# Three chunks of 4, 5 and 7 blocks in the input projection, the first norm's root ahead of the conditioning sums, lambdas and bounds at the beginning

## The chip, the cores and the metric

The kernel runs on one core of a Trainium2 chip. The metric is the device time of one execution in microseconds. The kernel before takes 1553.63 us, the median of 3 runs (1551.51 to 1554.83).

## The reference

One encoder layer on 256 rows of width 2048, all in float32:

```
cond = silu(c);  mod = cond @ w_mod + b_mod          # w_mod is 2048 x 12288, 101 MB
sh1, sc1, gt1, sh2, sc2, gt2 = split(mod, 6)
u = rms_norm(x, norm1_g) * (1 + sc1) + sh1
aq|ak|av|rq|rf|ri|rg|ga|gr = u @ w_in                # w_in is 2048 x 11264
lam = exp(sum(lq1*lk1)) - exp(sum(lq2*lk2)) + lam_init
ya = differential attention(aq, ak, av, lam)
yr = gated linear recurrence(rq, rf, ri, rg; lower bounds from softmax(lb_logits))
m = sigmoid(ga) * (ya @ w_att_out) + sigmoid(gr) * (yr @ w_rec_out)
x = x + gt1 * (m @ w_o);  u2 = rms_norm(x, norm2_g) * (1 + sc2) + sh2
x = x + gt2 * ((silu(u2 @ w_ffn_gate) * (u2 @ w_ffn_up)) @ w_ffn_down);  out = rms_norm(x, final_g)
```

Each weight is used once, on 256 rows. The output must hold float32 accuracy, so each matrix product is made of three passes (below).

## The kernel before

Rows of x lie in two halves of 128; the 2048 inputs of each product are 16 blocks of 128. A weight tile w is loaded by a DMA of SP's queue (L220), cast by ScalarE to a rounded high half wh (L235), and VectorE subtracts it to get the low half wl (L237). The activations have halves uH and uL likewise. TensorE then issues three matmuls of 512 columns for each block and each half of the rows: wh with uH, wl with uH, wh with uL (L245 to L247), so 6 matmuls a block, into PSUM tiles named acc.

The first norm needs its scale and shift, which are themselves a product with w_mod (sc1, sh1). VectorE makes them, in mod_cols: tiles wm of w_mod are loaded, multiplied by a column of cond and summed into two tiles modc (L398 and L402; ci is 0 for the shift and 1 for the scale); TensorE sums these over the partitions by matmuls against a column of ones, into pmc (L330; each is two records in the trace); VectorE adds the bias and the norm's weight (sh_col, sc_col, L421 to L423); ScalarE makes u (L368) and uH (L378), VectorE uL (L379).

The first 7 groups of columns of w_in (rf, rq, ri, aq, ak, av, rg, in 14 groups of 512 columns) do not wait for all 16 blocks. The blocks are cut into chunks, kchunks: 3, 4, 5 and 4 blocks (L45). For each chunk all 14 groups are computed with that chunk's blocks alone. After the first chunk ScalarE copies the sums to tiles part (L452); after each later chunk VectorE adds the new sums to them (L454). While chunk n runs, the scale and shift for chunk n+1 are made beside it, spread over the groups by pace["cond"] (AHEAD is 1.15, so a little ahead of even). Chunk 0's are made before anything else. Its wm tiles, and half of the next chunk's, lie in buffers of the big pool (27 of 4 KB a partition); all others share 3 buffers of their own, as the weights w have 3.

Blocks of a chunk beyond a multiple of 4 are loaded apart: 3 blocks in a load of 128x3x512; a single block in a load of 128x1024, shared by two groups.

Ahead of all this the kernel loads c, turns it into columns by TensorE, and makes cond = silu(c) (sigmoid on ScalarE, L131). load_rows loads six small parameters by ScalarE's queue. rstd1 sums the squares of x on ScalarE (L338) and takes the root by Newton steps on VectorE (L350, L198 to L213); norm1 scales x by it (L357), TensorE turns it (L360), ScalarE stores xT (L361). small_params makes lower bounds and lambda; its four loads of lambda stand in SP's queue (L179).

A scheduler of the language orders the instructions of each engine by its own model of times, within the data's dependencies. An engine executes its list in that order and waits at the first instruction that is not ready. tc.issue_after(ins) adds a rule to that ordering: what is issued under it, on the engine of ins, stands behind ins in the list. Each DMA has one of 8 slots (DMAHW0 to DMAHW7), given out in turn to all queues; a DMA waits until the one before it in its slot has landed.

Of the kernel before, what the change touches and what calls it, by code (L numbers as in the profile page):

```python
# [12 lines left out]
AF = mybir.ActivationFunctionType  # L13
# [5 lines left out]
P = 128  # L19
D = 2048  # L20
S = 256
KT = D // P
# [19 lines left out]
UACT, YACT = True, True  # L42
XAT, XAT2 = 2, 14
PACE2, PACE3, PACES, PACE1 = 0.7, 1.6, 2.2, 1.5
kchunks = [(0, 3), (3, 4), (7, 5), (12, 4)]  # L45


AQ, AK, AV, RQ, RF, RI, RG, GA, GR = 0, 1024, 2048, 3072, 4096, 5120, 6144, 7168, 9216
# [3 lines left out]
def block_kernel(  # L52
# [7 lines left out]
    nc = tc.nc  # L60
    x, out = x[0], out[0]
# [16 lines left out]
    def bank(name):  # L78
        return ps.tile([P, 512], F32, tag="ps", name=name)

    def tmpt(name, n=512, dt=F32):
        return tmp.tile([P, n], dt, tag=f"t{n}", name=name, bufs={512: NT, 256: 2}[n])
# [39 lines left out]
    def quarter(tiles, g):  # L122

        return tiles[g // 2][:, (g % 2) * NG:(g % 2 + 1) * NG]
# [3 lines left out]
    pcond = bank("pcond")  # L128
    nc.tensor.transpose(out=pcond[:, :KT], in_=crow[:KT, :], identity=ident[:KT, :KT])
    cond = const.tile([P, KT], F32, name="cond")  # L130
    nc.scalar.activation(cond, pcond[:, :KT], AF.Sigmoid)  # L131
    nc.vector.tensor_mul(out=cond, in0=cond, in1=pcond[:, :KT])

    nrow, nbrow = 57, 6 * KT
# [2 lines left out]
    g1c, g2c, lbl, gnc = cols[:, 0:16], cols[:, 16:32], cols[:, 32:48], cols[:, 48:56]  # L137
# [24 lines left out]
    def small_params():  # L162

        m8 = small.tile([P, HEADS], F32, tag="s8", name="lbm")
        nc.vector.tensor_max(out=m8, in0=lbl[:, 0:8], in1=lbl[:, 8:16])
        e = small.tile([P, 2, HEADS], F32, tag="s16", name="lbe")
        for i in range(2):
            nc.vector.tensor_sub(out=e[:, i], in0=lbl[:, 8 * i:8 * i + 8], in1=m8)
        nc.scalar.activation(e, e, AF.Exp)
        z = small.tile([P, HEADS], F32, tag="s8", name="lbz")  # L170
        nc.vector.tensor_add(out=z, in0=e[:, 0], in1=e[:, 1])
        nc.vector.reciprocal(out=z, in_=z)
        nc.vector.tensor_mul(out=lbc, in0=e[:, 0], in1=z)
        nc.vector.tensor_scalar(out=omlb, in0=lbc, scalar1=-1.0, scalar2=1.0, op0=ALU.mult, op1=ALU.add)
        nc.vector.tensor_scalar_mul(out=subc, in0=cols[:, 56:57], scalar1=1.0 - LAM_INIT)

        lv = tmpt("lv", S).rearrange("p (i d) -> p i d", d=64)
        for i, ap in enumerate((lambda_q1, lambda_q2, lambda_k1, lambda_k2)):
            nc.sync.dma_start(out=lv[:, i, :], in_=ap.to_broadcast([P, 64]))  # L179
        nc.vector.tensor_mul(out=lv[:, 0:2], in0=lv[:, 0:2], in1=lv[:, 2:4])  # L180
        ls = small.tile([P, 2], F32, tag="s2", name="ls")
        nc.vector.reduce_sum(out=ls, in_=lv[:, 0:2], axis=AX.X)
        nc.scalar.activation(ls, ls, AF.Exp)

        nc.vector.tensor_sub(out=lam[:, 0:1], in0=ls[:, 0:1], in1=ls[:, 1:2])
        nc.vector.tensor_scalar_add(out=lam[:, 0:1], in0=lam[:, 0:1], scalar1=LAM_INIT)
        nc.vector.tensor_scalar_mul(out=lam[:, 1:2], in0=lam[:, 0:1], scalar1=-1.0)

    last_rstd = []
# [110 lines left out]
    def halves(tiles):  # L300

        return lambda k, ts: tiles[k // 4].rearrange("p (k s) -> p k s", s=S)[:, k % 4, ts]
# [34 lines left out]
    def square_sum(dst, src):  # L337
        return nc.scalar.activation(junk[:, :src.shape[-1]], src, AF.Square, accum_out=dst)  # L338

    xT, uH_t, uL_t = [], [], []  # L340
    xTv, uH, uL = halves(xT), halves(uH_t), halves(uL_t)

    def rstd1(xt):

        s8 = small.tile([P, 2, 4], F32, tag="s8", name="ssq")
        for t in range(2):
            for g in range(4):
                square_sum(s8[:, t, g:g + 1], quarter(xt[t], g))
        s2 = small.tile([P, 2], F32, tag="s2", name="ssq1")
        nc.vector.reduce_sum(out=s2, in_=s8, axis=AX.X)  # L350
        return rstd_of(s2, 2, D, "n1")
# [29 lines left out]
    def mod_loads(nk):  # L381
        wid = nk * P
        kk = min(KT, 1024 // wid)
        return [(q, min(kk, KT - q)) for q in range(0, KT, kk)]

    def mod_cols(k0, nk, chunk, gcol, src, H, L, after=None, room=0, lag=0):

        wid = nk * P  # L390
        a = [tmp.tile([P, 1024], F32, tag="modc", name=f"modc{ci}", bufs=2) for ci in range(2)]
        waiting = []

        def sums(q, kk, ci, w):
            for j in range(kk):
                s1, d = cond[:, q + j:q + j + 1], a[ci][:, :wid]
                if q + j == 0:
                    first = nc.vector.tensor_scalar_mul(out=d, in0=w[:, j], scalar1=s1)  # L398
                    if after is not None:
                        tc.add_manual_dep(first.ins, after.ins.name, NOSYNC, reason="the norm goes first")  # L400
                else:
                    nc.vector.scalar_tensor_tensor(out=d, in0=w[:, j], scalar=s1, in1=d, op0=ALU.mult, op1=ALU.add)  # L402

        for q, kk in mod_loads(nk):
            for ci in range(2):
                waiting.append((q, kk, ci, load_mod(q, kk, (chunk + ci) * D + k0 * P, wid, q >= room)))
                if ci == 0:
                    yield
            while len(waiting) > (lag if q < room else 0):
                sums(*waiting.pop(0))  # L410
            yield
        for w in waiting:
            sums(*w)
        p = bank("pmc")
        for ci in range(2):
            col_sum(p, ci * nk, a[ci], nk)
        for _ in range(GAP if chunk else GAP1):
            yield
        ks = slice(k0, k0 + nk)
        bc = [bcols[:, (chunk + ci) * KT + k0:(chunk + ci) * KT + k0 + nk] for ci in range(2)]  # L420
        nc.vector.tensor_add(out=sh_col[:, ks], in0=p[:, 0:nk], in1=bc[0])  # L421
        nc.vector.tensor_add(out=sc_col[:, ks], in0=p[:, nk:2 * nk], in1=bc[1])
        nc.vector.scalar_tensor_tensor(out=sc_col[:, ks], in0=sc_col[:, ks], scalar=1.0, in1=gcol[:, ks], op0=ALU.add, op1=ALU.mult)  # L423
        if src is not None:
            for k in range(k0, k0 + nk):
                modulated(src(k, slice(0, S)), k, H, L)
# [30 lines left out]

    def mods1(ci):
        k0, nk = kchunks[ci]
        return mod_cols(k0, nk, 0, g1c, xTv, uH, uL, room=(KT, KT // 2, 0, 0)[ci], lag=(0, 4, 0, 0)[ci])  # L460

    def chunk_cols(ci):
        k0, nk = kchunks[ci]
# [166 lines left out]
    def attention(hh):  # L630
# [6 lines left out]
        for t in range(2):  # L637
# [50 lines left out]
            yield  # L688

    first = mods1(0)  # L690
    for _ in range(XAT):
        next(first)
    x1 = load_x()
    load_rows()
    r1 = rstd1(x1)
    for _ in range(XAT2):
        next(first, None)
    xT += bigt("xT", n=4)
    for g in range(4):
        norm1(x1, r1, g)  # L700
# [4 lines left out]
    for ci in range(len(kchunks)):  # L705
        chunk_cols(ci)
        if ci == 0:
            small_params()
            make_masks()


# [213 lines left out]
```

## Time and profile before

| what | value |
| --- | --- |
| median of 3 runs | 1553.63 us |
| profiled execution: time, span | 1557.73 us, 1555.5 us |
| TensorE matmul busy | 1504.1 us (97%) |
| VectorE busy | 1101.3 us (71%) |
| ScalarE busy | 733.9 us (47%) |
| moved by DMA | 373.67 MB, mean 240 GB/s |

The span is the time from the first to the last instruction of the profiled execution. Matmuls are pipelined, so a busy TensorE is not one at its peak: starts have to be counted. A group of instructions goes by its line in the kernel, the engine and the operation. The name in brackets behind an idle time is what ended the wait, by the semaphores.

### The profile page before, as it was taken

What the parts mean: (1) busy time and instruction counts of PE and PEld (TensorE: products, weight loads), DVE (VectorE), ACT (ScalarE), POOL (GpSimd) and SP (SyncE); (2) the same over time, 40 slices, a digit from 0 to 9 for tenths busy, and PEclk for the clock granted to TensorE, in tenths of its full rate; (3) what the DMA queues carried; (4) which work ended last, traced back from release to release, by engine and by line L of the source; (5) the groups of instructions that cost most, each with busy time, mean ns of one, the idle gap of its engine ahead of it and who ended that gap; (6) DMA issues with size and microseconds to landing.
All of it is one profiled execution on the core that took longest, in us unless ns stands there. A gap on an engine that the chain in (4) does not pass through costs nothing.

```text
span 1555.5 us, 18285 instructions
## 1 busy us (share of the span) xinstructions
PE 1504.1 (97%) x6931; PEld 1236.5 (79%) x6931; DVE 1101.3 (71%) x1439; ACT 733.9 (47%) x1016; POOL 10.5 (1%) x40
## 2 busy tenths in 40 slices
PE   3999999999999999999989999999999999999997
PEld 2778788888878778788878888888888888888885
DVE  5879898688877687988469878879555555555555
ACT  5653433524566764444355555444433444444443
POOL 1000000000000000000000000000000000000000
PEclk9999999999999999999999999999999999999998
DMA  9789898634664379899549998958655555556553
GB/s 319 268 296 338 276 322 289 208 126 158 228 246 160 111 279 323 317 323 339 194 145 333 329 323 288 317 195 312 214 191 190 190 188 190 190 189 210 196 192 105
DMA packets 175986, 373.67 MB, mean 240 GB/s; under 512 B 8429, under 2 KB 12694, under 8 KB 175898
## 3 DMA queue, kind: packets, MB, share of 16 engines
q1 hardware_dynamic: 175352, 371.90, 69.6%
q8 instruction: 54, 0.88, 0.2%
q10 hardware_dynamic: 546, 0.61, 0.1%
q14 instruction: 34, 0.28, 0.0%
HBM read 370.38 MB, written 2.10 MB: 239 GB/s over the span
## 4 chain that ended last, share of the span: by engine, by line
PE 79%; DVE 9%; DMA 6%; ACT 2%; issue 2%; SPq 0%; DVEq 0%; ACTq 0%
PE acc L246 24%; PE acc L247 24%; PE acc L245 24%; DMA wm<-in_w_mod_dram 5%; DVE wl L237 3%; DVE modc L402 2%; PE ptr L499 2%; PE pl L584 2%; PE pmc L330 1%; DVE gt L315 1%; DMA w<-in_w_in_dram 1%; DMA x<-in_x_dram 1%; DVE part L454 0%; ACT wh L235 0%; PE psc L647 0%
## 5 line engine op out<-in xcount | busy, mean ns | idle before, releaser
L235 ACT CAST wh<-w 128x1024 fp32r<-128x1024 f32 (+1 forms) x518 | 528.8, 1030 | 669.3 <-PE acc L247 568.0
L237 DVE TENSOR_TENSOR wl<-w,wh 128x1024 fp32r<-128x1024 f32 (+1 forms) x518 | 614.2, 1193 | 325.0 <-ACT wh L235 323.3
L246 PE MATMUL acc<-wl,uH 128*128 128x512 f32 x704 | 278.2, 395 | 2.0 <-DVE wl L237 2.0
L245 PE MATMUL acc<-wh,uH 128*128 128x512 f32 x704 | 276.8, 396 | 3.2 <-ACT uH L378 1.9
L247 PE MATMUL acc<-wh,uL 128*128 128x512 f32 x704 | 277.4, 394 | 0.0
L246 PE MATMUL acc<-wl,u2H 128*128 128x512 f32 x704 | 274.4, 390 | 2.8 <-DVE wl L237 2.8
L245 PE MATMUL acc<-wh,u2H 128*128 128x512 f32 x704 | 275.3, 391 | 1.6 <-ACT u2H L786 1.6
L247 PE MATMUL acc<-wh,u2L 128*128 128x512 f32 x704 | 274.9, 391 | 0.0
L402 DVE SCALAR_TENSOR_TENSOR modc<-wm,cond,modc 128x512 f32<-128x512 f32 (+3 forms) x210 | 168.1, 822 | 18.4 <-DMA wm<-in_w_mod_dram 17.5
L246 PEld LDWEIGHTS acc<-wl,uH 128*128 128x128 f32 x704 | 133.3, 189 | 33.5 <-DVE wl L237 5.3
L245 PEld LDWEIGHTS acc<-wh,uH 128*128 128x128 f32 x704 | 133.3, 189 | 30.8 <-ACT uH L378 2.0
L246 PEld LDWEIGHTS acc<-wl,u2H 128*128 128x128 f32 x704 | 132.2, 188 | 31.0 <-DVE wl L237 3.6
L247 PEld LDWEIGHTS acc<-wh,uL 128*128 128x128 f32 x704 | 133.2, 189 | 28.0 <-issue 0.6
L245 PEld LDWEIGHTS acc<-wh,u2H 128*128 128x128 f32 x704 | 132.2, 188 | 29.1 <-ACT u2H L786 1.9
L247 PEld LDWEIGHTS acc<-wh,u2L 128*128 128x128 f32 x704 | 132.2, 188 | 27.1 <-DVE u2L L787 0.2
L246 PE MATMUL acc<-wl,fH 128*128 128x512 f32 x352 | 137.4, 390 | 0.0
L247 PE MATMUL acc<-wh,fL 128*128 128x512 f32 x352 | 137.1, 390 | 0.0
L245 PE MATMUL acc<-wh,fH 128*128 128x512 f32 x352 | 137.0, 389 | 0.0
L315 DVE SCALAR_TENSOR_TENSOR gt<-wm,cond,gt 128x1024 f32<-128x1024 f32 x64 | 81.7, 1277 | 11.8 <-DMA wm<-in_w_mod_dram 11.5
L247 PEld LDWEIGHTS acc<-wh,fL 128*128 128x128 f32 x352 | 66.1, 188 | 14.0 <-issue 0.2
L246 PEld LDWEIGHTS acc<-wl,fH 128*128 128x128 f32 x352 | 66.1, 188 | 13.8 <-issue 0.2
L245 PEld LDWEIGHTS acc<-wh,fH 128*128 128x128 f32 x352 | 66.1, 188 | 13.7
(251 smaller groups left out, 1226.6 us busy)
## 6 DMA issues: line engine op xcount, KB each, us to landing
wm<-in_w_mod_dram SPq DMA_DIRECT2D x160, 512.0 KB, 6.2
w<-in_w_in_dram SPq DMA_DIRECT2D x74, 1024.0 KB, 5.5
w<-in_w_ffn_gate_dram SPq DMA_DIRECT2D x44, 1024.0 KB, 5.2
w<-in_w_ffn_up_dram SPq DMA_DIRECT2D x44, 1024.0 KB, 7.3
w<-in_w_ffn_down_dram SPq DMA_DIRECT2D x44, 1024.0 KB, 5.2
w<-in_w_o_dram SPq DMA_DIRECT2D x16, 1024.0 KB, 7.2
w<-in_w_in_dram SPq DMA_DIRECT2D x14, 768.0 KB, 7.7
wm<-in_w_mod_dram SPq DMA_DIRECT2D x32, 320.0 KB, 4.3
```

The lines of the kernel that those rows point to most:

```text
L235: nc.scalar.copy(out=wh, in_=src)
L237: nc.vector.tensor_sub(out=wl, in0=src, in1=wh.bitcast(F32))
L245: mm(po[t], aH(k, ts), h, start=first, stop=False)
L246: mm(po[t], aH(k, ts), lo, start=False, stop=False)
L247: mm(po[t], aL(k, ts), h, start=False, stop=last)
L315: nc.vector.scalar_tensor_tensor(out=a[i], in0=w[:, 0], scalar=cond[:, k:k + 1], in1=a[i], op0=ALU.mult, op1=ALU.add)
L330: mm(p[:, j0 + j:j0 + j + 1], a[:, j * P:(j + 1) * P], ones[:, 0:1], start=True, stop=True)
L402: nc.vector.scalar_tensor_tensor(out=d, in0=w[:, j], scalar=s1, in1=d, op0=ALU.mult, op1=ALU.add)
L499: nc.tensor.transpose(out=p[:, j * P:(j + 1) * P], in_=src[:, j * P:(j + 1) * P], identity=ident)
L584: mm(p[:, (4 * b + j) * 64:(4 * b + j + 1) * 64], kb[:, j, b * P:(b + 1) * P], qb[:, j, b, :, 1, :], start=True, stop=True)
```

## The change

The chunks become 4, 5 and 7 blocks instead of 3, 4, 5 and 4. The first norm's squares are issued behind the sigmoid on ScalarE; the conditioning sums from the third step of the generator on are issued behind the last Newton step on VectorE. small_params is split: lambdas() loads the lambdas by ScalarE's queue instead of SP's and makes lambda, small_params() the bounds; both are called ahead of norm1, under the same rule, instead of behind the first chunk.

```diff
-kchunks = [(0, 3), (3, 4), (7, 5), (12, 4)]
+kchunks = [(0, 4), (4, 5), (9, 7)]
...
-    nc.scalar.activation(cond, pcond[:, :KT], AF.Sigmoid)
+    cond_act = nc.scalar.activation(cond, pcond[:, :KT], AF.Sigmoid)
...
         nc.vector.tensor_scalar_mul(out=subc, in0=cols[:, 56:57], scalar1=1.0 - LAM_INIT)
 
+    def lambdas():
+
         lv = tmpt("lv", S).rearrange("p (i d) -> p i d", d=64)
         for i, ap in enumerate((lambda_q1, lambda_q2, lambda_k1, lambda_k2)):
-            nc.sync.dma_start(out=lv[:, i, :], in_=ap.to_broadcast([P, 64]))
+            nc.scalar.dma_start(out=lv[:, i, :], in_=ap.to_broadcast([P, 64]))
...
-        return mod_cols(k0, nk, 0, g1c, xTv, uH, uL, room=(KT, KT // 2, 0, 0)[ci], lag=(0, 4, 0, 0)[ci])
+        return mod_cols(k0, nk, 0, g1c, xTv, uH, uL, room=(KT, KT // 2, 0)[ci], lag=(0, 4, 0)[ci])
...
-    r1 = rstd1(x1)
-    for _ in range(XAT2):
-        next(first, None)
+    with tc.issue_after(cond_act.ins):
+        r1 = rstd1(x1)
+    for i in range(XAT2):
+        with tc.issue_after(last_rstd[0]) if i >= 2 else ExitStack():
+            next(first, None)
+    with tc.issue_after(last_rstd[0]):
+        lambdas()
+        small_params()
...
         chunk_cols(ci)
         if ci == 0:
-            small_params()
             make_masks()
```

Lines below L45 move by two in the changed kernel (L402 becomes L404, L237 becomes L239, and so on), those behind the calls by more.

The list of VectorE before, where the first norm's root is taken (ssq1 is the sum of squares, n1 the root's steps, modc0 and modc1 the conditioning sums of the first chunk):

```order
L402 SCALAR_TENSOR_TENSOR modc1_103<-wm00_176,cond_90,modc1_103 128x384 [waits DMAHW0_49]
L350 TENSOR_REDUCE ssq1_142<-ssq_133 128x2 [waits Activation_49]
L402 SCALAR_TENSOR_TENSOR modc1_103<-wm00_176,cond_90,modc1_103 128x384 [waits DVE_49]
L198 TENSOR_SCALAR n1v_144<-ssq1_142 128x2 [waits DVE_49]
L402 SCALAR_TENSOR_TENSOR modc0_102<-wm00_182,cond_90,modc0_102 128x384 [waits DMAHW1_49]
L202 TENSOR_SCALAR n1y_145<-n1v_144 128x2 [waits DVE_49]
L205 TENSOR_SCALAR n1h_149<-n1v_144 128x2
L402 SCALAR_TENSOR_TENSOR modc0_102<-wm00_182,cond_90,modc0_102 128x384 [waits DVE_49]
```

The same place in the changed kernel, from the last sum ahead of the root:

```order
L404 SCALAR_TENSOR_TENSOR modc1_103<-wm00_168,cond_90,modc1_103 128x512 [waits DVE_49]
L352 TENSOR_REDUCE ssq1_142<-ssq_133 128x2 [waits Activation_49]
L200 TENSOR_SCALAR n1v_144<-ssq1_142 128x2 [waits DVE_49]
L204 TENSOR_SCALAR n1y_145<-n1v_144 128x2 [waits DVE_49]
L207 TENSOR_SCALAR n1h_149<-n1v_144 128x2
L205 TENSOR_SCALAR n1y_145<-n1y_145 128x2 [waits DVE_49]
L213 TENSOR_TENSOR n1q0_151<-n1y_145 128x2 [waits DVE_49]
L214 TENSOR_TENSOR n1q0_151<-n1q0_151,n1h_149 128x2 [waits DVE_49]
L215 SCALAR_TENSOR_TENSOR n1y0_152<-n1q0_151,n1y_145 128x2 [waits DVE_49]
```

The root's steps stood one by one between sums; now they stand together, and 24 of the 32 sums stand behind them.

The list of VectorE before, where the first chunk's scale and shift are done and its first weights are split:

```order
L402 SCALAR_TENSOR_TENSOR modc1_103<-wm00_216,cond_90,modc1_103 128x384 [waits DVE_49]
L421 TENSOR_TENSOR sh_col_101<-pmc_298,bcols_94 128x3 [waits PE_49]
L422 TENSOR_TENSOR sc_col_100<-pmc_298,bcols_94 128x3
L423 SCALAR_TENSOR_TENSOR sc_col_100<-sc_col_100,cols_93 128x3 [waits DVE_49]
L237 TENSOR_TENSOR wl_326<-w_322,wh_324 128x1024 [waits DMAHW3_49,Activation_49]
L379 TENSOR_TENSOR uL0_294<-u_308,uH0_290 128x256 [waits Activation_49]
```

The same place in the changed kernel:

```order
L423 TENSOR_TENSOR sh_col_101<-pmc_322,bcols_94 128x4 [waits PE_49]
L424 TENSOR_TENSOR sc_col_100<-pmc_322,bcols_94 128x4
L425 SCALAR_TENSOR_TENSOR sc_col_100<-sc_col_100,cols_93 128x4 [waits DVE_49]
L187 TENSOR_TENSOR lam_98<-ls_228 128x1 [waits Activation_49]
L171 TENSOR_TENSOR lbz_240<-lbe_236 128x8 [waits Activation_49]
L188 TENSOR_SCALAR lam_98<-lam_98 128x1 [waits DVE_49]
L172 RECIPROCAL lbz_240<-lbz_240 128x8 [waits DVE_49]
L189 TENSOR_SCALAR lam_98<-lam_98 128x1 [waits DVE_49]
L173 TENSOR_TENSOR lbc_95<-lbe_236,lbz_240 128x8 [waits DVE_49]
L174 TENSOR_SCALAR omlb_96<-lbc_95 128x8 [waits DVE_49]
L381 TENSOR_TENSOR uL0_318<-u_334,uH0_314 128x256 [waits Activation_49]
```

Seven small steps of lambda and the bounds stand there now, and the low half of the weights (wl) stands behind the first two low halves of u. On ScalarE the cast of these weights stands behind the first two casts of u instead of ahead of them.

The queue of SP before, at the beginning of chunk 1 (w are weights of w_in, wm tiles of w_mod, lv the lambdas):

```order
L220 DMA wm_1012<-in_w_mod_dram 128x640 [waits DMAHW2_49,DVE_49]
L220 DMA wm_1016<-in_w_mod_dram 128x640 [waits DMAHW3_49,DVE_49]
L179 DMA lv_888<-in_lambda_q1_dram 128x64 [waits DMAHW0_49,DVE_49]
L179 DMA lv_888<-in_lambda_q2_dram 128x64 [waits DMAHW1_49]
L179 DMA lv_888<-in_lambda_k1_dram 128x64
L179 DMA lv_888<-in_lambda_k2_dram 128x64
L220 DMA w_1022<-in_w_in_dram 128x4x512 [waits DMAHW4_49]
L220 DMA wm_1056<-in_w_mod_dram 128x640 [waits DMAHW5_49]
```

The queue of SP in the changed kernel, in chunk 1:

```order
L222 DMA w_1586<-in_w_in_dram 128x4x512 [waits DMAHW3_49,Activation_49]
L222 DMA w_1628<-in_w_in_dram 128x1024 [waits DMAHW7_49,DMAHW4_49,DVE_49]
L222 DMA wm_1584<-in_w_mod_dram 128x896 [waits DMAHW0_49,DVE_49]
L222 DMA wm_1620<-in_w_mod_dram 128x896 [waits DMAHW1_49,DVE_49]
L222 DMA wm_1624<-in_w_mod_dram 128x896 [waits DMAHW2_49,DVE_49]
L222 DMA w_1632<-in_w_in_dram 128x4x512 [waits DVE_49]
```

The lambdas are gone from this queue (they are the third to sixth load of ScalarE's now), and chunk 1's weights of 4 + 1 blocks share the queue with conditioning tiles of 896 columns, for 7 blocks.

## Rows read from the trace of the kernel before

**Rows 1.** The page's engines: busy us, share of the span, instructions.

```profile
PE 1504.1 (97%) x6931; PEld 1236.5 (79%) x6931; DVE 1101.3 (71%) x1439; ACT 733.9 (47%) x1016; POOL 10.5 (1%) x40
```

**Rows 2.** Windows of the first three chunks: us from the start, length, busy time by engine.

```profile
40.19:97.35 57.16, 56.36 (x234) 45.65 (x235) 46.91 (x63) 35.29 (x55) 0.00 (x0) 1.00 0.88 305
97.35:178.80 81.45, 78.92 (x350) 63.19 (x348) 72.64 (x95) 32.52 (x41) 0.00 (x0) 1.00 0.87 299
178.80:276.50 97.70, 97.70 (x437) 81.03 (x435) 82.61 (x112) 40.90 (x52) 0.00 (x0) 0.98 0.87 302
```

**Rows 3.** Timeline of TensorE, 20 starts apart: start, length, instruction.

```profile
754.83 0.39 PE L245 MATMUL acc<-wh,mH 128*128 128x512 f32 x1
...
759.37 0.39 PE L247 MATMUL acc<-wh,mL 128*128 128x512 f32 x1
```

**Rows 4.** Timeline of TensorE: column sums after chunks 0 and 1.

```profile
97.35 1.84 PE L330 MATMUL pmc<-ones,modc 128*128 128x1 f32 x16
...
178.66 2.29 PE L330 MATMUL pmc<-ones,modc 128*128 128x1 f32 x20
```

**Rows 5.** Timeline of TensorE at the start of chunk 0.

```profile
35.69 2.56 PE L330 MATMUL pmc<-ones,modc 128*128 128x1 f32 x12
40.19 0.79 PE L245 MATMUL acc<-wh,uH 128*128 128x512 f32 x1 [1.94 <-ACT uH L378]
...
45.47 0.48 PE L245 MATMUL acc<-wh,uH 128*128 128x512 f32 x1
```

**Rows 6.** Timeline of TensorE behind the boundary of chunks 0 and 1.

```profile
104.46 0.50 PE L245 MATMUL acc<-wh,uH 128*128 128x512 f32 x1 [1.03 <-ACT part L452]
```

**Rows 7.** VectorE: groups by form (count, busy, mean ns, idle before), then timeline.

```profile
L402 DVE SCALAR_TENSOR_TENSOR modc<-wm,cond,modc 128x384 f32<-128x384 f32 x30 | 17.8, 614 | 2.2 <-DMA wm<-in_w_mod_dram 1.9
...
L402 DVE SCALAR_TENSOR_TENSOR modc<-wm,cond,modc 128x640 f32<-128x640 f32 x30 | 25.8, 879 | 4.5 <-DMA wm<-in_w_mod_dram 4.5
...
106.83 2.36 DVE L237 TENSOR_TENSOR wl<-w,wh 128x1024 fp32r<-128x1024 f32 x2 [0.97 <-ACT wh L235]
...
116.43 1.28 DVE L454 TENSOR_TENSOR part<-acc,part 128x512 f32<-128x512 f32 x2
```

**Rows 8.** Timeline of VectorE at the start.

```profile
18.35 0.15 DVE L350 TENSOR_REDUCE ssq<-ssq 128x2 f32<-128x8 f32 x1
...
25.56 6.00 DVE L402 SCALAR_TENSOR_TENSOR modc<-wm,cond,modc 128x384 f32<-128x384 f32 x10
...
38.36 0.15 DVE L422 TENSOR_TENSOR sc_col<-pmc,bcols 128x3 f32<-128x3 f32 x1
38.55 0.16 DVE L423 SCALAR_TENSOR_TENSOR sc_col<-sc_col,cols 128x3 f32<-128x3 f32 x1
```

**Rows 9.** By tile: x (squares, landing), then landing of rows and of lv.

```profile
L338 ACT ACTIVATE junk<-x x8: 629/629/644, 7.9 to 16.0; 128x512 f32<-128x512 f32 x8
...
DMA to landing us min/median/max: 7.9/8.3/8.7
...
DMA to landing us min/median/max: 4.8/4.8/4.9
...
DMA to landing us min/median/max: 2.8/2.9/2.9
```

**Rows 10.** Timeline of ScalarE at the start.

```profile
35.32 1.05 ACT L235 CAST wh<-w 128x1024 fp32r<-128x1024 f32 x1
...
39.74 0.69 ACT L378 CAST uH<-u 128x256 fp32r<-128x256 f32 x2
```

**Rows 11.** Windows of chunk 1, as rows 2; the last three columns: PEclk, DMA share, GB/s.

```profile
97.35:113.00 15.65, 14.62 (x73) 12.04 (x72) 11.57 (x22) 8.48 (x17) 0.00 (x0) 1.00 0.68 220
113.00:150.00 37.00, 36.30 (x159) 29.49 (x158) 35.46 (x43) 14.03 (x14) 0.00 (x0) 1.00 0.95 336
150.00:171.50 21.50, 20.70 (x87) 15.68 (x86) 19.03 (x24) 6.96 (x8) 0.00 (x0) 1.00 0.86 294
```

**Rows 12.** Waits of SP's queue, 97 to 179 us: waited for, total us, times, longest.

```profile
SPq L220 <- DVE lam L187: 5.1, 1, 5.1
```

## The prediction

> **What bounds the kernel now.** I read the page's engine line first: TensorE has matmuls in flight for 97% of the span [rows 1], so a microsecond counts only where TensorE starts late, waits or runs slowly. The windows by chunk come next [rows 2], since the change stays inside the input projection. Column sums of the conditioning (pmc) end each chunk's preparation; from one set to the next TensorE issues 234, 330 and 414 big matmuls in the built order. The reader needs their pace: twenty starts take 4.54 us [rows 3], 0.227 us each. Chunk 0 should then take 234 x 0.227 = 53.1 us and takes 57.16; chunk 1 should take 74.9 and 1.84 for its column sums [rows 4], 76.8, and takes 81.45; chunk 2 should take 94.0 and 2.1, 96.1, and takes 97.8 (from 178.66, where its column sums start). Lost: 4.1, 4.7 and 1.7 us. Those 10.5 us and the 40.19 us before the first big matmul [rows 5] are all that this change can touch much.
>
> What the losses are: the first 12 starts in chunk 0 take 5.28 us where 2.7 would do [rows 5], the pace of the lower of TensorE's two clock levels (1.2 GHz), though the granted clock is given as 1.00 [rows 2]: 2.6 us. The other 1.5 there are waits for weights. In chunk 1, 1.2 us go at the boundary, where TensorE waits for ScalarE's evacuation [rows 6]; 3.5 us go later, with the lambda loads at their head. Chunk 2's 1.7 us are again the lower clock (granted 0.98 [rows 2]), after 2.3 us of column sums [rows 4].
>
> **The start.** The first chunk has 4 blocks: its 32 products are 512 columns wide, not 384. One of 384 takes 614 ns and one of 640 takes 879 [rows 7], so one of 512 takes 746; neighbours overlap by about 0.08 us, which leaves 0.67 us. Eight stand ahead of the root, 24 behind it.
>
> When does the root start? Its reduction began at 18.35 us [rows 8]. ScalarE then did eight squares from 7.9, when x landed, to 16.0 [rows 9], and lost time to a second function table and to the parameter rows. Now the sigmoid comes first, but so do the parameter rows' loads, and the last of them waits for the second x load, which itself now waits for the first conditioning load. I put that landing at about 10 us: x began to land at 7.9 with less ahead of it. Four squares of 0.76 us (0.63 [rows 9] and a read-out), the copies of the parameter columns at about 14.4, four squares more: the reduction starts at 17.7. It is 16 if nothing is waited for. It is 20.7 if the second x load, issued at about 4.7, takes the 8.3 us that x's loads took [rows 9], lands at 13 and shifts all this by 3. The root has 13 dependent steps; a dependent step follows in 0.19 us (38.36 to 38.55 [rows 8]), so 2.6 us. In before it lay between sums and took 7.2 us, from 18.35 to 25.56.
>
> The last x load waits for the first lambda row. Small loads beside big ones took 4.8 us to land, in a quieter stretch 2.9 [rows 9]: issued at 2, the lambda row is there at 4.9 to 6.8, before the second x load has landed, so I add nothing. The Trainium skill ("DMA: Bandwidth & Descriptors", Queues, rings and completion order) says that a DMA's semaphore write lands only after that engine's earlier writes, across its queues. By that rule the lambda row completes behind both conditioning loads, at the late end of those two figures or after it; the two rows agree in direction, and the sum would be up to 1.9 us more.
>
> So the root ends at 20.3; 24 sums take 16.1, two lambda steps between them 0.4: 36.8. The last four column sums are 8 records of 0.213 us (2.56 us for 12 [rows 5]): 38.5. Scale columns 0.3 us later, 38.8, against 38.55 before [rows 8]. Earlier transposes thus buy nothing: they used to end shortly before the sums were reduced (35.69 [rows 5]), and now VectorE alone is late. Behind the scale, the weights' cast used to lie ready (35.32 [rows 10]); now it is queued behind both casts of u. Those ended at 40.43 [rows 10], 1.88 us after the scale step; with the cast, 2.85. First matmul: 38.8 + 2.85 = 41.65, 1.5 us later than 40.19. Its low half needs 1.23 us more on VectorE, while two matmuls at the lower clock cover 0.85: 0.4 us of waiting, where before had 0.2. **Start: +1.7 us** (bounds 0 and +4.7, by the root's start). Seven small steps for lambdas and bounds lie behind the scale, beside ScalarE's 1.88 us: nothing; without that cover, 7 x 0.19 = 1.3.
>
> **Chunk 0 and its end.** Groups grow from 18 to 24 matmuls, 5.4 us, with the same three weight buffers, so a load has 11 us of lead instead of 8. I count 0.5 us of the 1.5 us of waits (bounds 0 and 2): **-1.0**. Its column sums stand in two sets of 5, 46 and 24 matmuls ahead of the chunk's end, instead of one set 18 ahead. The 1.2 us boundary wait has 5.4 us of cover instead of 4.1: **-1.2** (0 to -1.2).
>
> **Chunk 1, the dear one.** It now prepares 7 blocks. From the second set to the next column sums there are 384 matmuls, 87.2 us. VectorE has in it 32 sums of 896 columns, 1.06 us each (879 + 265 - 80 ns), 33.9; low halves of 64 blocks at 0.572, 36.6 (pairs 1.13 [rows 7], singles 0.6); additions for 12 groups at 1.2 [rows 7], 14.4; low halves of u, 1.8. That makes 86.7 us, 99%. The same count for before's chunk 1 gives 25.6 + 31.1 + 15.6 + 2.4 = 74.7 of 74.9. VectorE is just as full, for longer.
>
> The loads: from the first 896-column load to the last, SP issues 32 x 0.459 MB and 14.1 MB of weights, 28.8 MB. About 85 us are there for them. What rate will they get? At 336 GB/s (113 to 150 us [rows 11]) 85.8 us, a wait of 1; at 294 (150 to 171.5 [rows 11]) 98, a wait of 13. Both stretches together give 321, a wait of 5. I take 325, 89 us, a wait of 4, nearest to both stretches together and a little better. The reason is that 97 to 113 us ran at 220 GB/s [rows 11]: there SP stood behind the lambda loads and for 5.1 us behind lambda's last step [rows 12]. That block is gone from the stretch. So 3.5 us of loss become 4: **+0.5** (bounds -2.5 and +9.8).
>
> **The clock.** Sixteen records of column sums at 97.35 took 1.84 us and the pace held; twenty at 178.66 took 2.29 and it fell [rows 4]. Two sets of 10 records should not make it fall, 28 in a row should: 2.2 us for 1.7 (bounds 0 and 2.6): **+0.5**.
>
> The last chunk, of 7 blocks, has no conditioning beside it, and the recurrence finishes inside it; VectorE drops 28 additions of 0.6 us, 17 us, which hide behind matmuls in before and so give nothing (0 to -1.5).
>
> **Sum.** 1.7 - 1.0 - 1.2 + 0.5 + 0.5 = +0.5 us. The profiled execution took 1557.73 us, its span and 2.2 around it, so 1558.2; the median of the runs shown is 1553.63, 4.1 lower. Forecast: 1554.1 us, own range 1551 to 1557.
>
> **Rivals.** *The loads fall behind.* One mechanism: in chunk 1 conditioning has three buffers, SP waits in order, and each late load holds weights too. From below 317 GB/s the wait passes 6 us and the kernel is slower by more than 3.1 us; at 294 it is 13, 9.3 more than I count: 1563.4. For it: 294 was the rate in the last third of before's chunk 1, and VectorE is 99% full. Against it: 336 held for 37 us beside an equally full VectorE.
>
> *The loads keep up.* With the lambda block gone the rate stays at 336: the wait is 1 us, 3 less; with another 1 us from VectorE's missing additions 1550.1 us. For it: the same row. Against it: the first sums then meet a full VectorE anyway.
>
> *The root is late.* The second x load lands at 13 us, the reduction starts at 20.7, the start costs 4.7 instead of 1.7: 1557.1. For it: 8.3 us for each of x's loads. Against it: those had 2.9 MB issued at once, and now a load finds at most two others ahead.
>
> **How the numbers follow.** Forecast 0.45, loads behind 0.25, loads in step 0.25, root late 0.05. About 0.2%, 3.1 us, can be told from no change here. The first gives mostly no change with a little on both sides; the second is slower for the most part; the third straddles the lower bound. That makes faster 0.26, no change 0.45, slower 0.29. The range goes from 1548.5, below the case in which loads keep up, to 1561.5, most of the way to 294 GB/s.
>
> **What would show it.** Right: the first big matmul at about 41.7 us, behind the weights' cast; the reduction at 17.7 and the transposes done by 32; no dip in the load rate just after the first boundary; a rate of about 325 GB/s in chunk 1 with some 4 us of TensorE waits, most of them for low halves; a fall of the clock after the second boundary only. Wrong: a first matmul before 40 or after 44 us; chunk 1 without waits or with over 7 us of them; or a change of more than 2 us behind 400 us, which I hold to be untouched.

## The result, and the profile after

The changed kernel takes 1565.66 us (median of 4 runs, 1562.38 to 1567.49) against 1554.23 (4 runs, 1551.51 to 1557.60) for the kernel before, run beside it on the same chip: a ratio of 1.0070, 95% interval 1.0044 to 1.0097. It is slower; the forecast was 1554.1, range 1548.5 to 1561.5.

The two profiled executions lie closer together than the medians. The one after took 1562.38 us, the lowest of its runs, span 1560.2; the one before took 1557.73, above the highest of the runs beside it. So the traces hold 4.7 of the 11.4 us; two more profiles of the change (after_again, big_26 below) show what varies.

The page's engine line after, to set beside [rows 1]:

```profile
PE 1502.3 (96%) x6931; PEld 1235.2 (79%) x6931; DVE 1083.5 (69%) x1376; ACT 726.0 (47%) x1009; POOL 10.7 (1%) x40
```

TensorE is busy 2 us less in a span 4.7 longer, and VectorE 18 us less, most of it the 28 dropped additions (54.9 us before, 38.0 after). Nothing became faster by it. Now the start: VectorE's timeline (start, length, instruction, idle time before it and what ended it), beside [rows 8].

```profile
17.84 0.16 DVE L352 TENSOR_REDUCE ssq<-ssq 128x2 f32<-128x8 f32 x1 [0.22 <-ACT junk L340]
...
20.21 0.16 DVE L215 SCALAR_TENSOR_TENSOR n1y<-n1q,n1y 128x2 f32<-128x2 f32 x1
20.29 14.00 DVE L404 SCALAR_TENSOR_TENSOR modc<-wm,cond,modc 128x512 f32<-128x512 f32 x21
...
39.15 0.16 DVE L425 SCALAR_TENSOR_TENSOR sc_col<-sc_col,cols 128x4 f32<-128x4 f32 x1
```

The root starts at 17.84 (before: 18.35), is done 2.5 us later, and the sums run behind it in one piece. ScalarE's timeline, beside [rows 10], with the first square at its head, and TensorE's first big matmul, beside [rows 5]:

```profile
10.40 0.63 ACT L340 ACTIVATE junk<-x 128x512 f32<-128x512 f32 x1 [5.16 <-DMA x<-in_x_dram]
...
40.40 0.69 ACT L380 CAST uH<-u 128x256 fp32r<-128x256 f32 x2
41.00 1.04 ACT L237 CAST wh<-w 128x1024 fp32r<-128x1024 f32 x1
```

```profile
42.09 1.22 PE L247 MATMUL acc<-wh,uH 128*128 128x512 f32 x2 [3.25 <-ACT wh L237]
```

The cast of the weights now stands behind both casts of u, and TensorE's first big matmul waits for it: 42.09 us instead of 40.19.

Next the first boundary, from TensorE's timeline (beside [rows 6]) and ScalarE's:

```profile
122.41 0.39 PE L249 MATMUL acc<-wh,uL 128*128 128x512 f32 x1
125.30 0.50 PE L247 MATMUL acc<-wh,uH 128*128 128x512 f32 x1 [2.50 <-ACT part L454]
```

```profile
117.73 1.09 ACT L370 ACTIVATE u<-xT,sh_col,sc_col 128x256 f32<-128x256 f32 x2 [3.36 <-DVE sc_col L425]
...
124.15 0.61 ACT L237 CAST wh<-w 128x512 fp32r<-128x512 f32 x1
124.67 2.02 ACT L454 COPY part<-acc 128x512 f32<-128x512 f32 x4
```

ScalarE works without a pause from 117.73 to 124.67 on u for five blocks and on weights; only then come the four copies that give TensorE its accumulators back. In before the same list, for four blocks, ran from 99.69 to 103.84:

```profile
99.69 1.09 ACT L368 ACTIVATE u<-xT,sh_col,sc_col 128x256 f32<-128x256 f32 x2 [2.13 <-DVE sc_col L423]
...
103.84 2.02 ACT L452 COPY part<-acc 128x512 f32<-128x512 f32 x4
```

Then chunk 1. I measure a chunk between two sets of column sums (pmc), because the built order tells how many big matmuls lie between them. Here it is 384, as forecast. At 0.227 us [rows 3] they take 87.17 us, and the second set itself 1.17. The two rows of TensorE:

```profile
116.05 1.17 PE L332 MATMUL pmc<-ones,modc 128*128 128x1 f32 x10
...
213.51 3.59 PE L332 MATMUL pmc<-ones,modc 128*128 128x1 f32 x28
```

From start to start are 97.46 us, 9.1 more than 88.34. The boundary's stop (122.41 to 125.30, less one step) is 2.7 of it, so 6.5 us are lost inside chunk 1. Windows of it (length, busy time of PE, PEld, DVE, ACT, POOL, granted clock, DMA share, GB/s), to read beside [rows 11]:

```profile
117.00:133.00 16.00, 13.50 (x60) 10.88 (x61) 13.74 (x21) 11.06 (x20) 0.00 (x0) 1.00 0.79 287
133.00:170.00 37.00, 36.03 (x157) 28.89 (x156) 31.68 (x36) 13.50 (x16) 0.00 (x0) 1.00 0.91 324
170.00:213.00 43.00, 39.58 (x171) 31.48 (x170) 39.14 (x43) 12.30 (x14) 0.00 (x0) 1.00 0.93 322
...
117.00:213.00 96.00, 89.11 (x384) 71.24 (x385) 84.56 (x98) 36.86 (x50) 0.00 (x0) 1.00 0.90 317
```

None of these windows has 336 GB/s, and the first 16 us have 287. Who is short of what shows in ScalarE's waits (100 to 215 us: total, times, longest) and in three rows of the timeline:

```profile
ACT wh L237 <- DMA w<-in_w_in_dram: 54.2, 13, 7.0
```

```profile
173.30 2.01 ACT L237 CAST wh<-w 128x1024 fp32r<-128x1024 f32 x2 [4.23 <-DMA w<-in_w_in_dram]
181.50 2.52 ACT L237 CAST wh<-w 128x1024 fp32r<-128x1024 f32 x3 [6.20 <-DMA w<-in_w_in_dram]
```

```profile
178.98 0.50 PE L248 MATMUL acc<-wl,uH 128*128 128x512 f32 x1 [2.14 <-DVE wl L239]
```

TensorE's own row names VectorE (wl); one step back ScalarE has no weights to cast, for 4 to 7 us at a time, because they have not landed. The releaser that TensorE's wait names is here only the last link. The total of 54.2 us is no measure of the loss, though. A second profile of the change (after_again) has 30.9 us there and loses more in chunk 1, 10.2 us, and before has 45.0 in the same stretch and loses 4.6 in its chunk 1:

```profile
ACT wh L235 <- DMA w<-in_w_in_dram: 45.0, 14, 5.8
```

That the loads are the cause is shown only by the experiments below.

Behind the 28 column sums the clock falls, as forecast: granted 0.83 over the next 20 us, and in the first of them TensorE's starts are 0.43 us apart instead of 0.227, the lower of its two levels (1.2 GHz).

```profile
213.00:233.00 20.00, 20.00 (x89) 16.87 (x89) 13.66 (x22) 13.78 (x23) 0.00 (x0) 0.83 0.66 236
```

```profile
218.38 0.63 PE L249 MATMUL acc<-wh,uL 128*128 128x512 f32 x1
218.81 0.63 PE L248 MATMUL acc<-wl,uH 128*128 128x512 f32 x1
```

### The profile page after: what moved, and what is told of

Same layout as the page of the kernel before. It is cut to its first block, busy times and chain, and to the rows that moved or that the text cites. A ratio compares the mean times of both kernels' runs of the same rounds, so it can differ in the third digit from the quotient of the medians.

```text
span 1560.2 us, 18240 instructions
## 1 busy us (share of the span) xinstructions
PE 1502.3 (96%) x6931; PEld 1235.2 (79%) x6931; DVE 1083.5 (69%) x1376; ACT 726.0 (47%) x1009; POOL 10.7 (1%) x40
## 4 chain that ended last, share of the span: by engine, by line
PE 83%; DVE 7%; DMA 4%; ACT 3%; issue 2%; SPq 0%; ACTq 0%; DVEq 0%
PE acc L247 26%; PE acc L248 26%; PE acc L249 26%; DMA wm<-in_w_mod_dram 2%; DVE wl L239 2%; PE ptr L501 2%; DVE modc L404 2%; PE pl L586 2%; DMA w<-in_w_in_dram 1%; ACT wh L237 1%; PE pmc L332 1%; ACT junk L340 1%; PE psc L649 0%; PE prow L327 0%; DMA x<-in_x_dram 0%
## 5 line engine op out<-in xcount | busy, mean ns | idle before, releaser
L239 DVE TENSOR_TENSOR wl<-w,wh 128x1024 fp32r<-128x1024 f32 (+1 forms) x518 | 614.5, 1193 | 344.0 <-ACT wh L237 339.2
L237 ACT CAST wh<-w 128x1024 fp32r<-128x1024 f32 (+1 forms) x518 | 529.7, 1030 | 682.3 <-PE acc L249 585.4
L404 DVE SCALAR_TENSOR_TENSOR modc<-wm,cond,modc 128x512 f32<-128x512 f32 (+3 forms) x180 | 161.1, 925 | 22.8 <-DMA wm<-in_w_mod_dram 22.3
```

The lines of the kernel that those rows point to most:

```text
L237: nc.scalar.copy(out=wh, in_=src)
L239: nc.vector.tensor_sub(out=wl, in0=src, in1=wh.bitcast(F32))
```

## The experiments

The table has all runs, the change twice (after, after_again); the ratio is to the kernel before run beside it, whose median was 1554.23 to 1557.67. "Lost" is TensorE's time from the start of one set of column sums to the start of the next, around chunk 1, less the first set (by the length of its row) and less 0.227 us for each big matmul between: 384 of them, but 330 with the old plan, 408 in loads_cut and 336 in plan_4_4_8. It contains the boundary's stop where there is one.

```
kernel        median us  ratio   95% interval     first matmul  lost
before        1554.23                             40.19          4.6
after         1565.66    1.0070  1.0044..1.0097   42.09          9.1
after_again   1563.96    1.0062  1.0043..1.0081   42.64         10.2
chunks_only   1572.10    1.0105  1.0087..1.0122   44.78         13.1
start_only    1549.85    0.9968  0.9955..0.9981   39.17          1.2
lambda_only   1552.24    0.9980  0.9966..0.9993   42.59          1.2
sums_cut      1563.76    1.0050  1.0025..1.0074   42.89         10.4
loads_cut     1558.76    1.0028  1.0017..1.0038   42.32          2.6
plan_4_4_8    1565.97    1.0072  1.0052..1.0093   42.94         12.4
four_buffers  1560.83    1.0042  1.0025..1.0059   42.92         10.5
parts_first   1564.11    1.0043  1.0026..1.0061   42.60         12.6
big_26        1565.94    1.0058  1.0037..1.0080   42.79          9.6
start_four    1548.89    0.9946  0.9927..0.9966   39.77          0.3
```

### Which part costs, and which gains

chunks_only is the kernel before with the new plan alone; after_again is the change once more:

```
-kchunks = [(0, 3), (3, 4), (7, 5), (12, 4)]
+kchunks = [(0, 4), (4, 5), (9, 7)]
```

start_only is the change with the old plan, everything else kept. lambda_only is start_only without the two rules that queue squares and sums:

```
-    with tc.issue_after(cond_act.ins):
-        r1 = rstd1(x1)
-    for i in range(XAT2):
-        with tc.issue_after(last_rstd[0]) if i >= 2 else ExitStack():
-            next(first, None)
+    r1 = rstd1(x1)
+    for _ in range(XAT2):
+        next(first, None)
```

Expected of chunks_only: 

> Only the chunk plan changes (4, 5 and 7 blocks); the start and the lambdas are as before. Theory L (the second chunk, which prepares 7 blocks, is where the time goes): 8 to 11 us slower than before, some 6 us of TensorE waits between the second and third set of column sums. Theory S (the new order of the start costs it): not more than 4 us slower than before.

Of start_only: 

> The four chunks of before with the new start and the lambdas moved. Theory L: within 3 us of before, rather faster (the lambda block of 1 to 2 us in the second chunk is gone). Theory S: 6 us or more slower than before, with a first big matmul after 42 us.

Of lambda_only: 

> The four chunks and the root's place of before; only lambdas and bounds are moved to the beginning. Theory L: 1 to 3 us faster than before, no dip of the load rate between 97 and 113 us. Theory S in the form that the four small loads at the beginning hold x back: slower than before by 1 to 3 us, the squares ending over 1 us later.

Of after_again: 

> The changed kernel once more, for its spread: both theories expect 7 to 12 us more than before in the median, and a profile in which the waits of the second chunk differ from the first profile by several us while the start agrees within 0.5 us.

Measured beside a kernel before of 1555.38: the plan alone costs 16.7 us, the rest alone gains 5.5, together they cost 8.6. The whole loss is the plan's (14.1 us on top of the rest). Three expectations were missed in size: chunks_only costs more than the 8 to 11 of theory L, with its first matmul 4.6 us later and 13.1 us lost around chunk 1; start_only gains more than 3; and the two profiles of the change differ by 1.1 us in chunk 1, not by several, and by 0.55 at the start. The rows, first chunks_only, then start_only, then lambda_only: TensorE's first big matmul and the column sums around chunk 1.

```profile
44.78 0.79 PE L245 MATMUL acc<-wh,uH 128*128 128x512 f32 x1 [1.94 <-ACT uH L378]
...
121.67 1.17 PE L330 MATMUL pmc<-ones,modc 128*128 128x1 f32 x10
...
223.07 3.18 PE L330 MATMUL pmc<-ones,modc 128*128 128x1 f32 x28
```

```profile
39.17 0.80 PE L247 MATMUL acc<-wh,uH 128*128 128x512 f32 x1 [3.01 <-ACT uH L380]
...
94.47 1.84 PE L332 MATMUL pmc<-ones,modc 128*128 128x1 f32 x16
...
172.39 2.29 PE L332 MATMUL pmc<-ones,modc 128*128 128x1 f32 x20
```

```profile
42.59 0.80 PE L247 MATMUL acc<-wh,uH 128*128 128x512 f32 x1 [1.93 <-ACT uH L380]
...
98.27 1.84 PE L332 MATMUL pmc<-ones,modc 128*128 128x1 f32 x16
...
176.22 2.29 PE L332 MATMUL pmc<-ones,modc 128*128 128x1 f32 x20
```

The rules on the root are worth 3.4 us at the start in the profiles (42.59 to 39.17), 2.4 in the medians. Against before they win only 1.0 there, because the lambdas' move by itself makes the start 2.4 us later (40.19 to 42.59): in lambda_only the root ends at 26.8 us instead of 25.6, and lambda's steps on ScalarE, a table load of 1.28 us among them, stand between the copies of xT. What the move wins, it wins in chunk 1: 330 matmuls between the sets take 77.9 us instead of 81.3 [rows 4], 1.2 us lost instead of 4.6, in start_only and in lambda_only. Windows of start_only, in the stretches of [rows 11]:

```profile
94.50:111.00 16.50, 16.50 (x82) 13.95 (x81) 12.79 (x20) 11.23 (x18) 0.00 (x0) 1.00 0.85 301
111.00:148.00 37.00, 36.03 (x159) 29.50 (x159) 35.40 (x43) 13.71 (x13) 0.00 (x0) 1.00 0.89 320
148.00:172.00 24.00, 24.00 (x108) 19.87 (x107) 24.00 (x29) 8.45 (x8) 0.00 (x0) 1.00 0.91 321
```

With the lambdas out of SP's queue the first 16.5 us load at 301 GB/s and the last 24 at 321; before had 220 and 294. lambda_only, with the lambdas out of the queue too, has 273 and 303 in these stretches and loses no more than start_only. So the dip that theory L had gone is only smaller there. These chunks nearly kept TensorE's pace, so their rates are close to what the chunk asked for; the 294 too may be that, and not what loads get at worst.

### Loads or VectorE: what holds chunk 1 back

sums_cut cuts VectorE's sums for the 7 blocks to 384 of 896 columns and leaves the loads; loads_cut leaves out half of the conditioning loads for the 7 blocks, 16 of 32, and keeps the sums. Of both edits the main part:

```
-                s1, d = cond[:, q + j:q + j + 1], a[ci][:, :wid]
+                cut = 384 if chunk == 0 and k0 == 9 else wid
+                s1, d, w_ = cond[:, q + j:q + j + 1], a[ci][:, :cut], w[:, j, :cut]
```

```
-                waiting.append((q, kk, ci, load_mod(q, kk, (chunk + ci) * D + k0 * P, wid, q >= room)))
+                if ci == 0 or not (chunk == 0 and k0 == 9):
+                    tile_w = load_mod(q, kk, (chunk + ci) * D + k0 * P, wid, q >= room)
+                waiting.append((q, kk, ci, tile_w))
```

Expected of sums_cut: 

> The changed kernel, with the sums for the 7-block chunk over 384 of their 896 columns (the other columns' scale and shift are left out, repeated from the first); the loads stay. VectorE saves 32 x 0.53 = 17 us in the second chunk. Theory V (VectorE, 97 to 99% full there, makes TensorE wait): the waits between the second and third column sums, 7 to 11 us in two profiles, fall below 2 us, and the kernel is 5 us or more faster than the changed one. Theory D (the loads cannot be delivered in time): they stay above 5 us, the time within 3 us of the changed kernel's 1564 us.

Of loads_cut: 

> The changed kernel, with one load in place of two for the 7-block chunk: the scale's sums read the shift's weights (the scale's own weights are left out); the number of sums stays. 7.3 MB less in the second chunk. Theory D: the waits there fall below 2 us, 5 us or more faster than the changed kernel. Theory V: they stay above 5 us, the time within 3 us of 1564 us.

One window of each over chunk 1, sums_cut first:

```profile
118.00:214.00 96.00, 89.07 (x383) 71.27 (x383) 70.05 (x100) 37.10 (x50) 0.00 (x0) 0.98 0.87 316
```

```profile
118.00:216.00 98.00, 95.50 (x434) 79.20 (x434) 89.62 (x105) 43.23 (x56) 0.00 (x0) 1.00 0.80 278
```

In sums_cut VectorE is down to 70 of 96 us and nothing is won: 10.4 us lost, 316 GB/s. In loads_cut VectorE is full (90 of 98), 278 GB/s suffice, and of the loss only the boundary is left: 408 matmuls and a set are 93.8 us, and from 117.49 to 213.91 it took 96.4. Its median lies 5.2 us under that of after_again. ScalarE's waits there, over the stretch in which after has 54.2 us for weights:

```profile
ACT wh L237 <- PE acc L249: 40.5, 26, 2.1
ACT wh L237 <- DMA w<-in_w_in_dram: 13.2, 7, 3.4
```

Now ScalarE waits for TensorE, as it should. The loads are what chunk 1 lacks; a VectorE that is 90% full does not hold it back. SP's queue does wait for VectorE's sums, which give the three conditioning buffers back (39.1 us from 117 to 214 us), but with the shorter sums of sums_cut it waits as long (42.9), so it is not the length of the sums that holds the queue. Whether the number of loads or their bytes are too many, loads_cut alone does not tell, since it takes away both.

### Other plans, more buffers

plan_4_4_8 moves one block from chunk 1 to the last:

```
-kchunks = [(0, 4), (4, 5), (9, 7)]
+kchunks = [(0, 4), (4, 4), (8, 8)]
```

> The changed kernel with chunks of 4, 4 and 8 blocks: the second chunk computes 4 blocks (76 us) and prepares 8. Theory D: 14.7 MB of weights and 16.8 of conditioning at 336 GB/s take 94 us, so 16 us or more of waits in the second chunk, and a time of 1570 to 1578 us. Theory V: sums of 1024 columns, 32 x 1.2 = 38 us, with 31 of low halves and 17 of additions make 88 us for 76, 12 us of waits. A chunk plan whose price is only the number of blocks in the last chunk would stay within 3 us of the changed kernel.

```profile
115.95 1.84 PE L332 MATMUL pmc<-ones,modc 128*128 128x1 f32 x16
...
206.46 3.63 PE L332 MATMUL pmc<-ones,modc 128*128 128x1 f32 x32
```

90.51 us for 336 matmuls and a set (78.1): 12.4 us lost, and no boundary stop among them. So the waits are 12.4 instead of 6.5. That is theory V's number (12) and not theory D's (16 or more), though sums_cut speaks against V; the loads' rate is the change's:

```profile
118.00:206.00 88.00, 80.48 (x334) 64.28 (x333) 81.93 (x87) 31.16 (x38) 0.00 (x0) 0.96 0.90 316
```

From set to set it is 317 GB/s, which makes 28.7 MB, less than the 31.5 that theory D counted. To keep TensorE's pace, 78.1 us, it would have needed 367 GB/s; the change moves 31.0 MB from set to set at 318 and needed 351; start_only moves 24.6 MB, needed 321, got 316 and loses 1.2 us. The time, 1565.97, is the change's own and lies below the 1570 to 1578 that I expected of theory D: fewer bytes fell into the stretch, and the boundary costs nothing with four blocks of u, which I had not taken off.

four_buffers gives the conditioning a fourth buffer, at the cost of one large buffer; big_26 is its control, with the large buffer gone and no fourth:

```
-BIG = 27
-NW, NM, NH, SK = 3, 3, 4, 2
+BIG = 26
+NW, NM, NH, SK = 3, 4, 4, 2
```

Expected of four_buffers: 

> The changed kernel with 4 instead of 3 buffers for the conditioning's loads (and 26 instead of 27 big tiles, to make room). Theory B (the round trip through 3 buffers limits the loads): the waits in the second chunk fall by half or more, 4 us or more faster than the changed kernel. Theories D and V: within 3 us of it.

Of big_26: 

> The changed kernel with 26 instead of 27 of the large shared buffers, as in four_buffers, but with three conditioning buffers. It tells what of four_buffers (1560.83) was the fourth conditioning buffer. Theory: the large buffers are not short in the input projection, so this is the changed kernel again, 1563.96 within 1.5 us, with the 2.5 us boundary wait and the fall of the clock behind 28 column sums. Rival: the shared buffers order something else, and the boundary wait is gone here too: about 1561.

```profile
111.59 2.29 PE L332 MATMUL pmc<-ones,modc 128*128 128x1 f32 x20
...
211.58 1.62 PE L332 MATMUL pmc<-ones,modc 128*128 128x1 f32 x14
```

Here too 384 matmuls lie between, with 2.29 us for the set: 10.5 us lost, and this kernel has no boundary stop. The fourth buffer changes where the sums fall, not how long chunk 1 waits; the 4 us of theory B did not come. Against its control (1.0042 to 1.0058, intervals overlapping) no gain can be told; the control lies 2.0 us above after_again, where 1.5 was expected, has the boundary's stop and no fall of the clock. In this chunk, room for more loads ahead did not raise their rate: 309 GB/s from set to set.

### Mending the boundary

parts_first puts two steps between the column sums and u, so that two of the four copies stand ahead of u in ScalarE's list:

```
-GAP, GAP1, LATE = 1, 0, True
+GAP, GAP1, LATE = 1, 2, True
```

> The changed kernel, with two steps between the last conditioning sums of the first norm and their use. ScalarE's list then has two of the four copies of partial sums ahead of u of chunk 1, at the first boundary. The 2.5 us wait of TensorE on 'ACT part' is there in all runs of the plan 4, 5, 7. Theory Q (only the order of ScalarE's list makes it): the wait falls under 0.6 us and the time falls by 2 to 2.7 us, to 1561 to 1562 against 1563.96. Rival G (given back): the wait goes, but chunk 1 is paced by its loads at 317 GB/s, so TensorE comes 2.5 us earlier to weights that are not there earlier: the waits of chunk 1 grow by as much and the time stays within 1 us of 1563.96. Rival U (u is late too): the copies push u and its casts back by 1 us and TensorE waits for uH instead; the boundary still costs over 1.5 us.

TensorE's waits from 125 to 235 us (total, times, longest) have no entry for "part" any more, nor have those from 100 us on:

```profile
PE acc L248 <- DVE wl L239: 3.7, 5, 1.5
PE acc L247 <- ACT wh L237: 3.5, 2, 2.1
```

```profile
117.23 1.17 PE L332 MATMUL pmc<-ones,modc 128*128 128x1 f32 x10
...
218.13 3.98 PE L332 MATMUL pmc<-ones,modc 128*128 128x1 f32 x28
```

The boundary is mended, so theory U is out, and yet 12.6 us are lost up to the next set, against 9.1 to 10.2 with the stop in it. This profile took 1567.34 us, near the highest of its 12 runs. The median of 1564.11 is that of the change, as rival G had it. By its ratio, beside a slower kernel before (1557.67), it might be up to 3 us better, as theory Q had it, but the intervals overlap. That chunk 1 takes back what the boundary gives, TensorE only coming earlier to weights that are not there earlier, fits the profile and is not shown by the times.

### Something faster

start_four is start_only with the buffers of four_buffers.

> start_only (chunks of 3, 4, 5 and 4 blocks, the rest of the change kept; 1549.85) with four conditioning buffers and 26 large ones, as in four_buffers. Theory: what is left to win in its chunks 0 and 1 is 7.5 us of loss by index 564, of which about 2.6 is the clock at the start; four buffers took 3.1 us off the changed kernel, mostly the boundary and the clock, which start_only does not lose. So at most 1 us: 1549 to 1550. Rival: conditioning loads further ahead help every chunk: 1547 or less. Rival: more loads in flight delay the weights: 1551 or more.

From set to set, 95.63 to 172.69 us, 0.3 us are lost in chunk 1, the least of all. 1548.89 cannot be told from the 1549.85 of start_only, nor 0.9946 from 0.9968, whose intervals overlap. Both beat the kernel before and the change; the old plan with the rest of the change is the version to keep.

## Why the prediction was wrong, by its steps

**What failed: "Chunk 1, the dear one", and "Chunk 0 and its end" at its boundary.** The first was right in mechanism and wrong in size: a wait of 4 us, where 6.5 were lost. I had taken 325 GB/s, and the whole stretch had 317. By the prediction's relation 28.8 MB at 317 are 90.9 us, 5.9 more than the 85 there are. This agrees but proves little, since a stretch with waits in it has a lower rate whatever made them; that it was the loads is shown by sums_cut and loads_cut. The rival "the loads fall behind" is the case that came, and it deserved more than a quarter. Its point was put wrongly: by the prediction's own sums 317 makes the wait 1.9 us longer than counted, and 3.1 us slower than before need a rate under about 314. Against it I had set 336 for 37 us. But no whole chunk had that rate: from set to set the kernels that load for 7 or 8 blocks in full had 309 to 318, and the most of any was 323 (start_four). The 336 came after 16 us at 220, and lambda_only still has 329 after 273: one stretch is not the rate of a chunk. The Trainium skill ("DMA: Bandwidth & Descriptors", Specifications) gives about 358 GB/s as a core's share of the memory's bandwidth; an estimate by it would have been 80 us and no wait. The rows differ: 322 at a DMA share of 0.93. The measurement decides.

**The boundary** was to gain 1.2 us and cost 1.5 more than before: its stop is 2.7 us where before had 1.2. I counted the cover (24 matmuls, 5.4 us) and not what has to fit under it: u for five blocks and their weights on ScalarE take 6.9 us from 117.73 to 124.67, where four blocks took 4.2 before. parts_first showed that the list's order is the cause. Whether the stop costs anything of its own while the loads lag stays open: its time did not fall clear of the spread.

**The start** was right: the reduction at 17.84 (17.7 forecast), the root done at 20.3, scale at 39.15 (38.8), first matmul at 42.09 (41.65) behind the weights' cast; +1.9 us for +1.7. What I did not see is that the larger first chunk spoils it: with 3 blocks the same start ends at 39.17, 1.0 earlier than before. "Earlier transposes thus buy nothing" was wrong of the root's rule in itself: with the new plan and the start of before (chunks_only) the first matmul comes at 44.78. The lambda rows, by the view of their tile:

```profile
L181 ACTq DMA_DIRECT2D lv<-in_lambda_q_dram x2: 453/474/496, 1.8 to 2.3; - x2
...
DMA to landing us min/median/max: 4.6/4.6/4.7
```

The trace has the landing of two of the four. If the first, issued at 1.8 us, took 4.6 us as they did, it landed at about 6.4, nearer the late one of my two figures. The rule of the Trainium skill ("DMA: Bandwidth & Descriptors", Queues, rings and completion order), that a DMA's semaphore write lands only after earlier writes of its DMA engine, had pointed to the late end; the row agrees as far as it goes. The last x load, which waits for that row, was issued at 6.6 us, right behind the one before it, so the 1.9 us that this could have cost did not appear.

**Chunk 0:** from 42.09 to the second set at 116.05 are 73.96 us, less 312 x 0.227 and one set of 1.17: 2.0 lost instead of 4.1. That is -2.1 for the -1.0 counted; in after_again it is about -1. Part of the surplus is luck: the first 12 starts took 4.63 us here, 5.28 before and 5.51 in after_again.

**The clock:** after the second boundary it fell, 2.9 us for 2.2 counted. The rule behind it, that the number of column sums decides, is not borne out: 20 of them brought the fall in before and start_four and none in start_only, 28 brought it in after and none in big_26, whose order is the same there.

```profile
172.40:192.00 19.60, 19.60 (x98) 16.58 (x97) 17.17 (x28) 11.32 (x19) 0.00 (x0) 1.00 0.75 263
```

```profile
215.07 3.18 PE L332 MATMUL pmc<-ones,modc 128*128 128x1 f32 x28
218.11 0.72 PE L247 MATMUL acc<-wh,uH 128*128 128x512 f32 x2
```

**The lambdas** got no term of their own; I let their gain offset the 7 blocks. Apart, they are large and of opposite sign: 3.4 us won in chunk 1 by the one, about 8 lost by the other (1.2 to 9.1, boundary included).

**"Untouched behind 400 us"** was wrong, though little of it is left in the sum. Counting TensorE's starts, the 1401st big matmul is at 407.78 us before and at 416.81 after, the last at 1544.44 and 1548.91: for the same 4647 steps 1136.7 and 1132.1 us, 4.6 less. Ahead of it, from 278.10 us before (422 steps) and 233.49 after (644 steps), the time beyond 0.227 us a step is 33.9 and 37.1, 3.2 more. That the wide last chunk takes up recurrence work that stood behind it before would explain both; it is not tested. Together that is -1.4 where I had counted nothing. Of the 4.6, some is this profile of before: the three others with the old plan take 1133.7 to 1135.2 us for these steps, the eight with 4, 5 and 7 blocks 1130.8 to 1132.5.

In the profiles, then: 1.9 - 2.1 + 1.5 + 3.0 + 1.2 = +5.5 by terms, and -1.4 behind them: 4.1 of the 4.7 us between the spans. The remaining 6.7 of the medians' 11.4 us is that one profile was the lowest of its kernel's runs and the other the highest. The runs of the change spread over 5 us, and between two profiles of it the loss in chunk 1 differs by 1.1 (9.1 and 10.2), that in chunk 0 by 1.2 and the start by 0.55. What makes the loads of one run quicker than those of another stays open.

## What to carry to other kernels

Where transfers set the pace, work out bytes over time for each stage of a new plan and set it against a rate that a whole stage sustained, not against the best stretch of one: a burst that follows a blocked queue is no promise. A wait removed ahead of such a stage may be given back in it. An edit that unblocks a queue and an edit that asks more of it should be priced apart, since they can cancel in the sum and leave the good one unseen; here the unblocking itself had a price at the start that only lambda_only shows. Where work on an engine's list grows with a chunk, count the list against its cover, not the cover alone.

## What the runs showed of the hardware

From set to set around chunk 1 the eight profiles that load for 7 or 8 blocks in full had 309 to 318 GB/s at DMA shares of 0.87 to 0.90, whatever was changed on VectorE, in the buffers or at the boundary. The fall of TensorE's clock behind single-column matmuls came and went at equal counts, and between after and big_26 in equal order (granted 0.83 in the 20 us from 213, 1.00 in the 20 us from 218.1); when it came early, the 28 column sums themselves took 3.59 (after) and 3.98 us (parts_first) instead of 3.18 (big_26).
